# Sliding windows by DMA alone: 13 staged batches instead of 11, copies in 32 KB packets, and an exact last store

## The chip, the core and the metric

The kernel runs on one core of one Trainium2 chip. The metric is the device time of one execution in microseconds (us); lower is better. Three executions of the kernel before took 764.2, 765.02 and 766.24 us, so its median is 765.02 us. The profile comes from one further execution, which took 772.19 us.

## What is computed

Each of 32 batches of 4096 rows by 256 float32 values is cut into 127 windows of 64 rows, each window starting 32 rows behind the one before:

```python
batch, length, dim = (32, 4096, 256)
window_size, stride = 64, 32
n_windows = (length - window_size) // stride + 1      # 127
for i in range(n_windows):
    start = i * stride
    result[:, i] = x[:, start:start + window_size].copy()
```

No arithmetic is done. A batch is 128 blocks of 32 rows (one block is 32 KB). Window i is block i followed by block i+1, 64 KB in all. So every block but the first and the last of a batch is written twice: once as the second half of a window, once as the first half of the next. The input has 128 MB, the output 254 MB.

## The kernel before

Everything is done by DMAs on two rings: SP (SyncE) issues on one, which the profile calls q1, and ACT (ScalarE) on the other, q10. No compute engine touches the data. All DMAs go through `start` (L59), so line 60 stands for each of them; `parts=2` limits a packet to 32 KB, without it a packet may have 64 KB.

There are two ways for a batch to get from the input to the output.

- **Copied batches** (21 of 32, on q1, `copy`, L91): straight from device memory to device memory, as whole windows. Three DMAs per batch: windows 0 to 63 (`WHOLE`) in packets of 64 KB, windows 64 to 111 in packets of 32 KB, and the last 15 windows in packets of 32 KB.
- **Staged batches** (11 of 32, the odd ones from 1 to 21, on q10): one load of the 128 blocks into an on-chip tile, one block for each partition (`load`, L73), then two stores of that tile (`store`, L81), one that puts block j into the first half of window j, one that puts it into the second half of window j-1. There are five tiles (`BUFS`).

Both stores use all 128 blocks although a batch has 127 windows. So each staged batch also writes half a window too much on either side: its last block lands in the first half of the first window of the next batch, and its first block in the second half of the last window of the batch before. These neighbours have to be right in the end, in one of two ways:

- Tied batches (0, 2, ... 16): SP waits until both staged neighbours are stored (`after_store`, L71) and copies the batch only then.
- Early batches (18, 20, 22): they are copied first of all, and the halves that staged neighbours spoil are copied once more at the end ("mends", L151 to L155, five DMAs of 32 KB, each as 16 packets of 2 KB). Before the mends SP waits for the stores of staged batches 17, 19 and 21 (L147 to L149) and for the early copies (L150). ACT likewise waits for the early copies ahead of the first store that spoils one (L142).

The order of q1 is made by `_order` (L99): early batches, then the free ones (23 to 31) with the tied ones put in between. It gives 18, 20, 22, 23, 0, 24, 2, 25, 4, 26, 6, 27, 8, 28, 10, 29, 12, 30, 14, 31, 16. The order of q10 is load 0, then for each n: load n+1, wait for load n, store n. A load into a used tile waits for the store that read it. At the end SP waits for all stores and copies (L156 to L158) and clears the semaphores.

Of the kernel before, what the change touches and what calls it, by code (L numbers as in the profile page):

```python
# [1 line left out]

# [4 lines left out]


STAGED = tuple(range(1, 22, 2))
BUFS = 5  # L10

WHOLE = 64

EARLY = (18, 20, 22)


class _Geometry:


    def __init__(self, x, out, W, S):  # L20
        self.B, self.L, self.D = x.shape
        self.x, self.out = x, out
        self.n_win = (self.L - W) // S + 1
        self.n_blk = self.L // S
        self.blk = S * self.D
        self.win = W * self.D
        assert W == 2 * S and self.n_blk == self.n_win + 1 == 128

    def src(self, b, block, dims):

        at = (b * self.n_blk + block) * self.blk
        return bass.AP(self.x.tensor, self.x.offset + at, dims)

    def dst(self, b, half, dims):

        at = b * self.n_win * self.win + half * self.blk
        return bass.AP(self.out.tensor, self.out.offset + at, dims)

    def rows(self, b, w0, n):

        s, d = [[self.blk, n], [1, self.win]], [[self.win, n], [1, self.win]]
        return self.dst(b, 2 * w0, d), self.src(b, w0, s)

    def half(self, b, half, block):

        dims = [[self.blk // 16, 16], [1, self.blk // 16]]
        return self.dst(b, half, dims), self.src(b, block, dims)


class _Kernel:  # L50
    def __init__(self, nc, g, tiles):
        self.nc, self.g, self.tiles = nc, g, tiles
        self.loaded = [nc.alloc_semaphore(f"loaded{i}") for i in range(len(tiles))]
        self.stored = [nc.alloc_semaphore(f"stored{i}") for i in range(len(tiles))]
        self.copied = nc.alloc_semaphore("copied")
        self.early = nc.alloc_semaphore("early")
        self.count = {}

    def start(self, engine, out, in_, sem, parts=1):  # L59
        engine.dma_start(out=out, in_=in_, max_dma_last_dim=65536 // parts).then_inc(sem, 16)  # L60
        self.count[id(sem)] = self.count.get(id(sem), 0) + 16

    def all_of(self, engine, sem):
        engine.wait_ge(sem, self.count[id(sem)])

    def slot(self, n):
        return divmod(n, len(self.tiles))

    def after_store(self, engine, n):
        turn, i = self.slot(n)  # L70
        engine.wait_ge(self.stored[i], 32 * (turn + 1))  # L71

    def load(self, n):  # L73

        g, (_, i) = self.g, self.slot(n)
        if n >= len(self.tiles):
            self.after_store(self.nc.scalar, n - len(self.tiles))
        src = g.src(STAGED[n], 0, [[g.blk, g.n_blk], [1, g.blk]])
        self.start(self.nc.scalar, self.tiles[i][:, :], src, self.loaded[i])

    def store(self, n):  # L81

        g, (turn, i) = self.g, self.slot(n)
        self.nc.scalar.wait_ge(self.loaded[i], 16 * (turn + 1))
        for half in (0, -1):
            dst = g.dst(STAGED[n], half, [[g.win, g.n_blk], [1, g.blk]])
            self.start(self.nc.scalar, dst, self.tiles[i][:, :], self.stored[i])

    def copy(self, b, sem):  # L91

        n, nc = self.g.n_win, self.nc
        self.start(nc.sync, *self.g.rows(b, 0, WHOLE), sem)
        self.start(nc.sync, *self.g.rows(b, WHOLE, n // 16 * 16 - WHOLE), sem, 2)
        self.start(nc.sync, *self.g.rows(b, n // 16 * 16, n % 16), sem, 2)


def _order(B):  # L99


    near = {b for s in STAGED for b in (s - 1, s + 1)}
    order = list(EARLY) + [b for b in range(B) if b not in near and b not in STAGED]
    tied = sorted(near - set(EARLY))
    n = len(order) + len(tied)
    for b in tied:
        behind = max(STAGED.index(s) for s in (b - 1, b + 1) if s in STAGED)
        order.insert(-(-(behind + 2) * n // len(STAGED)), b)
    return order


@with_exitstack
def kernel(
    ctx: ExitStack,
    tc: tile.TileContext,
    x: bass.AP,
    window_size: bass.AP,
    stride: bass.AP,
    out: bass.AP,
):  # L120
    nc = tc.nc
    W, S = int(window_size), int(stride)
    g = _Geometry(x, out, W, S)
    assert 0 not in STAGED and g.B - 1 not in STAGED
    pool = ctx.enter_context(tc.tile_pool(name="blocks", bufs=1))
    tiles = [pool.tile([g.n_blk, g.blk], x.dtype, name=f"xb{i}") for i in range(BUFS)]

    with tc.tile_critical():
        k = _Kernel(nc, g, tiles)
        for b in _order(g.B):  # L130
            if b not in EARLY:
                for s in (b - 1, b + 1):
                    if s in STAGED:
                        k.after_store(nc.sync, STAGED.index(s))
            k.copy(b, k.early if b in EARLY else k.copied)
        k.load(0)
        waited = False
        for n, s in enumerate(STAGED):
            if n + 1 < len(STAGED):
                k.load(n + 1)  # L140
            if not waited and (s - 1 in EARLY or s + 1 in EARLY):
                k.all_of(nc.scalar, k.early)  # L142
                waited = True
            k.store(n)


        for n, s in enumerate(STAGED):  # L147
            if s - 1 in EARLY or s + 1 in EARLY:
                k.after_store(nc.sync, n)  # L149
        k.all_of(nc.sync, k.early)  # L150
        for b in EARLY:  # L151
            if b - 1 in STAGED:
                k.start(nc.sync, *g.half(b, 0, 0), k.copied)
            if b + 1 in STAGED:
                k.start(nc.sync, *g.half(b, 2 * g.n_win - 1, g.n_blk - 1), k.copied)  # L155
        for n in range(len(STAGED)):  # L156
            k.after_store(nc.sync, n)
        k.all_of(nc.sync, k.copied)  # L158
        for sem in [*k.loaded, *k.stored, k.copied, k.early]:
            nc.sync.sem_clear(sem)  # L160


# [1 line left out]
_INS = ['x', 'window_size', 'stride']  # L164
_OUTS = [((32, 127, 64, 256), 'float32')]

_NUMBERS = {'window_size': 64, 'stride': 32}


# [26 lines left out]
```

## Time and profile before

| what | value |
|---|---|
| median of three executions | 765.02 us |
| the profiled execution | 772.19 us |
| its span in the profile | 770.4 us |
| bytes moved by the 16 DMA engines | 313.37 MB, 407 GB/s over the span |
| device memory read and written | 221.09 MB and 267.22 MB |
| stretch 20 to 735 us | DMA engines busy 100%, 416 GB/s |
| stretch 735 to 762 us | DMA engines busy 88%, 313 GB/s |
| stretch 762 to 770.4 us | DMA engines busy 9%, 35 GB/s |

The only busy instructions of a compute engine are four memsets of 0.1 us each, so the profile's list of groups and its chain are empty in this kernel. What can be read are the DMA part of the page (share of the 16 engines' time for each queue, and what they move in 40 slices), the issues with their time to landing, the waits of SP, and the trace's record of each packet, with its queue, size, start and duration.

By these records, a 32 KB packet takes 1211 ns at least, and 1213 ns in the median, on either queue. All 32 KB packets of q1 take 1254.2 ns in the mean (2646 packets), those of q10 1259.6 ns (4224), and the 64 KB packets of q1 2583.8 ns (1344); the commonest fast duration of these is 2418 ns. Each DMA also leaves a record of 4 bytes on each engine that it uses, 9 ns long. In the mean 16.05 packets are on record at a time in the middle of the run, where there are 16 engines.

### The profile page before, as it was taken

How to read it: one execution, taken by the hardware profiler on the slowest of the kernel's cores; microseconds unless marked ns; L12 is line 12 of the kernel's file. 1: busy time of each engine (PE TensorE's matmuls, PEld its weight loads, DVE VectorE, ACT ScalarE, POOL GpSimd, SP SyncE). 2: the span in 40 equal slices, each digit the busy share in tenths (PEclk: the TensorE clock that was granted, in tenths of full speed). 3: DMA queues.
4: the chain of work that ended last, by engine and by line, in shares of the span. 5: the costliest groups of instructions: out<-in, count | busy, mean ns of one | idle time of the engine just before them, and what ended most of it. 6: DMA issues, size and time to landing. Idle time of an engine off the chain costs nothing. (4 is left out here: it accounts for less than half of the span.)

```text
span 770.4 us, 179 instructions
## 1 busy us (share of the span) xinstructions
POOL 0.2 (0%) x4
## 2 busy tenths in 40 slices
POOL 0000000000000000000000000000000000000000
DMA  9999999999999999999999999999999999999994
GB/s 381 396 412 436 393 413 419 447 371 434 400 424 395 441 403 424 403 444 386 430 420 422 405 419 419 403 412 419 417 415 427 417 415 412 444 415 432 391 338 178
DMA packets 9890, 313.37 MB, mean 407 GB/s; under 512 B 1595, under 2 KB 1595, under 8 KB 1675
## 3 DMA queue, kind: packets, MB, share of 16 engines
q1 hardware_dynamic: 5137, 174.95, 55.3%
q10 hardware_dynamic: 4752, 138.41, 43.2%
q14 instruction: 1, 0.01, 0.0%
HBM read 221.09 MB, written 267.22 MB: 634 GB/s over the span
## 5 line engine op out<-in xcount | busy, mean ns | idle before, releaser
L177 POOL MEMSET const-bfloat16-1.0<- 128x1 bf16 x1 | 0.1, 101 | 0.0
L177 POOL MEMSET const-uint8-127<- 128x1 uint8 x1 | 0.1, 101 | 0.0
L177 POOL MEMSET const-float32-0.0<- 128x1 f32 x1 | 0.1, 98 | 0.2 <-issue 0.2
L177 POOL MEMSET const-float32-1.0<- 128x1 f32 x1 | 0.1, 98 | 0.0
## 6 DMA issues: line engine op xcount, KB each, us to landing
out_dram<-xb ACTq DMA_DIRECT2D x22, 4096.0 KB, 94.1
out_dram<-in_x_dram SPq DMA_DIRECT2D x21, 3072.0 KB, 118.5
xb<-in_x_dram ACTq DMA_DIRECT2D x11, 4096.0 KB, 129.6
out_dram<-in_x_dram SPq DMA_DIRECT2D x21, 960.0 KB, 124.8
out_dram<-in_x_dram SPq DMA_DIRECT2D x21, 111.2
out_dram<-in_x_dram SPq DMA_DIRECT2D x5, 32.0 KB, 23.1
```

What stands on the lines that cost most here:

```text
L177: nc = _bacc.Bacc("TRN2", target_bir_lowering=False, num_devices=1)
```

## The change

- `STAGED` becomes 1, 3, ... 25: 13 staged batches and 19 copied ones.
- `copy` loses `WHOLE`: one DMA for windows 0 to 111 and one for the last 15, both in packets of 32 KB.
- The last staged batch (25) is stored by a new function, `store_exactly`. It leaves out the half windows that do not belong to the batch: each half is stored by one DMA of 112 rows and one of 15.
- `EARLY` becomes 20, 22, 24, 26. The mends are issued as soon as the stores of staged batches 19, 21 and 23 have landed, one staged batch after the other, and no longer behind the store of the last staged batch. Batch 26 needs no mend, since 25 writes nothing beyond its own windows.
- `_order` puts a tied batch half a place later. The order of q1 is now 20, 22, 24, 26, 0, 27, 2, 4, 28, 6, 8, 10, 29, 12, 14, 30, 16, 18, 31.

```diff
-STAGED = tuple(range(1, 22, 2))
+STAGED = tuple(range(1, 26, 2))
-WHOLE = 64
-EARLY = (18, 20, 22)
+EARLY = (20, 22, 24, 26)
...
+        self.exact = nc.alloc_semaphore("exact")
...
+    def store_exactly(self, n):
+        g, (turn, i) = self.g, self.slot(n)
+        self.nc.scalar.wait_ge(self.loaded[i], 16 * (turn + 1))
+        whole = g.n_win // 16 * 16
+        for half in (0, 1):
+            for w, rows in ((0, whole), (whole, g.n_win - whole)):
+                dst = g.dst(STAGED[n], 2 * w + half, [[g.win, rows], [1, g.blk]])
+                src = self.tiles[i][w + half : w + half + rows, :]
+                self.start(self.nc.scalar, dst, src, self.exact)
+
     def copy(self, b, sem):
-        n, nc = self.g.n_win, self.nc
-        self.start(nc.sync, *self.g.rows(b, 0, WHOLE), sem)
-        self.start(nc.sync, *self.g.rows(b, WHOLE, n // 16 * 16 - WHOLE), sem, 2)
-        self.start(nc.sync, *self.g.rows(b, n // 16 * 16, n % 16), sem, 2)
+        whole = self.g.n_win // 16 * 16
+        self.start(self.nc.sync, *self.g.rows(b, 0, whole), sem, 2)
+        self.start(self.nc.sync, *self.g.rows(b, whole, self.g.n_win - whole), sem, 2)
...
-        order.insert(-(-(behind + 2) * n // len(STAGED)), b)
+        order.insert(-(-(2 * behind + 5) * n // (2 * len(STAGED))), b)
...
-            k.store(n)
-        for n, s in enumerate(STAGED):
+            (k.store if n < last else k.store_exactly)(n)
+        k.all_of(nc.sync, k.early)
+        for n, s in enumerate(STAGED[:last]):
             if s - 1 in EARLY or s + 1 in EARLY:
                 k.after_store(nc.sync, n)
-        k.all_of(nc.sync, k.early)
-        for b in EARLY:
-            if b - 1 in STAGED:
-                k.start(nc.sync, *g.half(b, 0, 0), k.copied)
-            if b + 1 in STAGED:
-                k.start(nc.sync, *g.half(b, 2 * g.n_win - 1, g.n_blk - 1), k.copied)
-        for n in range(len(STAGED)):
+            if s - 1 in EARLY:
+                k.start(nc.sync, *g.half(s - 1, 2 * g.n_win - 1, g.n_blk - 1), k.copied)
+            if s + 1 in EARLY:
+                k.start(nc.sync, *g.half(s + 1, 0, 0), k.copied)
+        for n in range(last):
             k.after_store(nc.sync, n)
+        k.all_of(nc.sync, k.exact)
         k.all_of(nc.sync, k.copied)
```

## The prediction

> **What bounds the kernel now.** I read first the page's DMA slices and its queues, since no compute engine works.
>
> ```profile
> DMA  9999999999999999999999999999999999999994
> GB/s 381 396 412 436 393 413 419 447 371 434 400 424 395 441 403 424 403 444 386 430 420 422 405 419 419 403 412 419 417 415 427 417 415 412 444 415 432 391 338 178
> ...
> q1 hardware_dynamic: 5137, 174.95, 55.3%
> q10 hardware_dynamic: 4752, 138.41, 43.2%
> ```
>
> All 16 DMA engines are busy to the end, and the queues hold 55.3 + 43.2 = 98.5% of their time. So time is bytes per engine times time per byte, and no wait counts unless it empties a ring. The slices swing between 371 and 447 GB/s: the time per byte is not constant. Next the waits of SP's queue:
>
> ```profile
> SPq L71 <- DMA out_dram<-xb: 601.5, 9, 97.0
> SPq L60 <- DMA out_dram<-xb: 85.8, 1, 85.8
> SPq L64 <- DMA out_dram<-in_x_dram: 26.3, 1, 26.3
> ```
>
> SP waits for stores nearly all the time, yet the engines never pause before 735 us: copies issued earlier cover these waits. Only the last 26.3 us (L64, all copies landed) is bare. The windows show the end:
>
> ```profile
> 20.00:735.00 715.00, 0.00 (x0) 1.00 1.00 416
> 735.00:762.00 27.00, 0.00 (x0) 1.00 0.88 313
> 762.00:770.40 8.40, 0.00 (x0) 1.00 0.09 35
> ```
>
> (columns: window, length, POOL, clock, DMA share, GB/s.) By the packet records q10's data ends at 736 us, q1's at 767.9; the engines end one by one, most between 758 and 764. One engine falls out at 710 already: it has no share in the DMAs of 15 windows.
>
> **The work of one engine**, before, for the 15 engines that set the end. A copied batch is 4 packets of 64 KB (64 windows / 16), 6 of 32 KB (48 x 2 / 16) and 2 (the last 15 windows): 512 KB. A staged batch is 8 + 8 + 8 packets of 32 KB: 768 KB. In all 21 x 512 + 11 x 768 = 19,200 KB, as 84 packets of 64 KB, 168 copied and 264 staged of 32 KB. At the mean durations: 84 x 2583.8 = 217.0, 168 x 1254.2 = 210.7, 264 x 1259.6 = 332.5, sum 760.3 us. The records overlap a little (16.05 at a time on 16 engines), so the true work is 760.3 / 1.003 = 758.1. The span closes: 2.2 until the first packet, 758.1, 7.6 from the mean engine to the last one with the small records, 2.5 from the last packet to the end: 770.4.
>
> At the fast durations the same packets would take 84 x 2.418 + 432 x 1.213 = 727.1 us. So 31 us are slowing, and the change is a trade of more bytes against less slowing.
>
> **Part 1, two batches from copied to staged.** 19 x 512 + 13 x 768 = 19,712 KB: one engine gets 512 KB more, all in 32 KB packets, 19 x 16 = 304 copied and 13 x 24 = 312 staged (the exact store has 14 + 2, as many as a plain one). Fast: 616 x 1.213 = 747.2 us, that is **+20.1 us**. Of these 0.7 us are the split of 84 large packets (2 x 1213 - 2418 = 8 ns each).
>
> **Part 2, the time of a packet.** From 25 to 735 us I cut the packet records into slices of 5 us. Where 64 KB packets are under 2% of the bytes (28 slices) the engines move 425.5 GB/s, where they are over 60% (35 slices) 400.7, all together 415.8. Staged bytes are 51% of the first kind and 32% of the second, so size and share of copies can't be told apart, but the change alters both towards the first kind: its staged share is 312/616 = 51%. 425.5 / 16 = 26.6 GB/s, or 1232 ns for 32 KB. A second reading: 32 KB packets that overlap no 64 KB packet take 1234.8 ns (copies) and 1246.3 (staged), mean 1240.6, over 1.003 1237. The lower end is the fast packet, 1213, which some stretches hold; the upper end is today's mean of all 32 KB packets, (304 x 1254.2 + 312 x 1259.6) / 616 / 1.003 = 1253. I take 1228, a little under both readings, because the copy's DMA of 64 windows, whose engines stand 4 windows apart, goes, and the engines of the new one stand 7 apart. 616 x 1.228 = 756.4: against the 758.1 of now **-1.7 us** for parts 1 and 2 together. Ends: 747.2 (-10.9) and 771.8 (+13.7).
>
> The row for that choice is 400.7 against 425.5 GB/s in the two kinds of slices. [...]
>
> **Part 3, the balance of the rings.** Each engine seems to take a packet of either ring in turn, the 4-byte record of each DMA too. Before, q1 has 21 x (12 + 3) = 315 turns, q10 11 x (24 + 3) = 297. So q10 should end with 18 turns of q1 left, some 14 data packets of 42.7 KB in the mean, 14 x 1.7 = 24 us; q1 ended 32 us behind q10, and q10 began 4.4 us ahead. The rule holds about. After: q1 19 x (16 + 2) + 5 mends x 2 = 352, q10 12 x 27 + 9 + 20 = 353. Both end together, with some 4 packets left for q10's early start. What the lone ring costs now: 32 KB packets behind 741 us take 1402 ns, 64 KB ones 3085. That is inside the means above, so nothing more is booked; the 7.6 us to the last engine I keep, with bounds of -4 and +4.
>
> **Part 4, waits.** q1 must never run dry while SP waits for a store. Store n ends at turn 27n + 36 of q10; when SP waits for it, 18 turns for each copy issued stand in q1. Batch 0 waits for store 0 with 72 turns issued against 36 run; the closest are batches 10, 14 and 18: 198 against 171, 252 against 225, 306 against 279. 27 turns are 24 packets, with as many of q10 between them: 48 x 1.23 = 59 us of cover. Without it, each microsecond of lateness leaves SP's ring empty and the staged ring alone. ACT's order is unchanged: while it waits for load n, store n-1 and load n+1 stand in the ring. Its wait for the early copies (four now, landing near turn 72, about 160 us) moves to n = 9, past 500 us, at nothing. Five buffers stay. SP issues 43 DMAs instead of 68 at about 0.6 us each, 15 us less on a queue that waits 600: nothing.
>
> **Part 5, mends and the last store.** Before, the five mends land 23.1 us after their issue, because q1's last copies stand ahead of them:
>
> ```profile
> out_dram<-in_x_dram SPq DMA_DIRECT2D x5, 32.0 KB, 23.1
> ```
>
> So their lateness costs nothing now. After, the last two are issued when store 11 lands, 20 turns before q10's end, about 16 x 2 x 1.23 = 39 us, behind some 15 turns of q1: they land ahead of the end. Were they still behind the last store, a bare landing of a few us would stand there. The exact store of 112 partitions is a form that the trace does not show. Its 16 packets per engine cost 1213 ns at least; the slowest stretch of 20 us has staged packets of 1356 ns: 16 x 0.128 = +2.0. I take +0.5, near a plain store. Small records: 101 an engine before, 84 after, at 9 ns: -0.2. [...]
>
> **Sum.** -1.7 + 0.5 - 0.2 = -1.4 us on the span: 769.0. The profiled execution took 772.19, 7.2 more than the median; I take the difference, not the level: 765.0 - 1.4 = **763.6 us**.
>
> **Rivals.**
> 1. *More bytes at the old pace* (slower). The slowing is of the memory, whatever the packet's size and ring, and 32 KB packets keep 1253 ns: 765.0 + 13.7 = 779 us. It decides from a mean of 1234 ns on (616 x 1.234 = 760.2, +2.1). For it: staged packets between none and eight 64 KB packets show 1246, 1240 and 1235 ns, no rise. Against it: 1272 ns with nine or more, and the 28 slices.
> 2. *Slowing nearly gone*: most packets at 1213: 765.0 - 10.9 = 754 us. For it: three quarters of the 32 KB packets are at this floor today, and the GB/s slices reach 447. Against it: the pure slices still average 425.5, not 432.
> 3. *The rings are not level* (slower): a ring runs out early because turns do not count as I think. If the 4-byte records took no turn, 304 stand against 312, 8 packets alone. If SP falls behind its 59 us, the hole is whole: 10 us would make 775. Against it: the 24 us worked out against 32 seen.
>
> **How the numbers follow.** A measurement of this kernel tells about 0.3% (2.3 us) from no change, so same is 762.7 to 767.3. My forecast has 0.55, split 0.25 faster, 0.165 same, 0.135 slower, since 1225 or 1236 ns would both fit it (762 to 769 us). Rival 1 0.20, slower; rival 2 0.18, faster; rival 3 0.07, of it 0.05 slower. Faster 0.25 + 0.18 = 0.43, same 0.165 + 0.02 = 0.19 (rounded up), slower 0.38. The range reaches close to rival 2's end and two thirds of the way to rival 1's: 753 to 775; the forecast's own is 757 to 769.
>
> **What would show it.** The page should have about 321.9 MB (19 x 8.32 + 13 x 12.58 + 0.2, less 0.1), 418 to 421 GB/s over the span, q1 and q10 near 49 and 50% of the engines, even slices without the swing of now, and both queues' data ending within 10 us of each other; the last bare wait of SP should be for the exact store or the copies, a few us. A 32 KB mean over 1240 ns shows rival 1, one at 1215 rival 2. Dips of the DMA share before 740 us would show rival 3. The prediction is wrong if the mean is near 1228 ns and the span still is not near 769: then the ends or a dry ring took the difference.

## The result, and the profile after

The changed kernel took 773.38 us (median of four executions, 772.0 to 774.32) beside 765.63 us of the kernel before (four executions, 764.2 to 766.87): a ratio of 1.010 with a 95% interval of 1.0073 to 1.0128. It is slower by 1%, clear of the interval. The forecast was 763.6 us and slightly faster; the measured time lies in its range of 753 to 775, on the other side of no change.

The DMA part of the page of the changed kernel, with its 40 slices, its queues (packets, MB, share of the 16 engines' time) and the traffic of device memory:

```profile
DMA  9999999999999999999999999999999999999994
GB/s 380 431 407 434 433 417 433 419 422 434 426 422 434 421 417 434 426 422 431 419 429 429 431 417 433 424 419 433 431 419 431 431 424 433 424 426 416 414 381 154
...
q10 hardware_dynamic: 5644, 163.51, 50.1%
q1 hardware_dynamic: 5575, 158.30, 48.4%
HBM read 212.83 MB, written 267.29 MB: 621 GB/s over the span
```

The swing of the slices is gone (407 to 434 in the middle, 371 to 447 before), and the rings share the engines evenly. In stretches of time:

```profile
20.00:735.00 715.00, 0.00 (x0) 1.00 1.00 425
735.00:753.00 18.00, 0.00 (x0) 1.00 0.95 383
753.00:762.00 9.00, 0.00 (x0) 1.00 0.87 288
762.00:772.50 10.50, 0.00 (x0) 1.00 0.12 42
```

(columns as in the prediction: window, length, POOL, clock, DMA share, GB/s.) The long stretch moves 425 GB/s where it moved 416, a gain of 2.2%, but 321.83 MB are to be moved instead of 313.37, 2.7% more. The end is still 30 us of falling rate. The waits of SP:

```profile
SPq L70 <- DMA out_dram<-xb: 506.9, 9, 59.8
SPq L59 <- DMA out_dram<-xb: 186.4, 3, 74.5
SPq L63 <- DMA out_dram<-xb: 35.9, 1, 35.9
...
SPq L63 <- DMA out_dram<-in_x_dram: 0.2, 1, 0.2
```

Before, the last bare wait was for the copies (26.3 us). Now it is for the exact store (35.9 us, where the prediction had a few us), and q1 is down 0.2 us later: counted in turns, the two rings end together, as foretold. Counted in data they do not. By the packet records the last 32 KB packet of a copy ends at 754.5 us and the last of the staged ring at 769.4; between them q1 has only its mends, 2 KB at a turn. The prediction had the two queues' data within 10 us of each other. By the same records the copies' 32 KB packets take 1238.1 ns in the mean, the staged ones 1240.9; those of the exact store alone 1416, the other staged ones 1231.5.

### The profile page after: what moved, and what is told of

It is laid out like the page before. It is cut to its first block, busy times and chain, and to the rows that moved or that the text cites. A ratio compares the mean times of both kernels' runs of the same rounds, so it can differ in the third digit from the quotient of the medians.

```text
span 772.5 us, 164 instructions
## 1 busy us (share of the span) xinstructions
POOL 0.2 (0%) x4
## 2 busy tenths in 40 slices
DMA packets 11220, 321.83 MB, mean 417 GB/s; under 512 B 1323, under 2 KB 1323, under 8 KB 1403
## 3 DMA queue, kind: packets, MB, share of 16 engines
q10 hardware_dynamic: 5644, 163.51, 50.1%
```

## The experiments

Theory A stood at first: the 512 KB more for each engine cost 20 us, and the slowing that the change removes is worth less than that. Theory A also took the profiled execution of the kernel before for a slow one. Its rivals: a profile adds 7 us to it (B), the 32 KB packets are the harm (C), the exact store is the harm (D). Ratios are to the kernel before on the same chip. The runs went to four chips, and on all of them the kernel before took 769.6 to 774.4 us.

### The kernel before once more (ctl_before)

No edit.

> The kernel before, unchanged, profiled once more. Theory A (the level of the one profiled execution was high: 31 us of slowing against some 24 in an ordinary one): the new profile has a span near 764 us, 32 KB packets of 1240 to 1250 ns and 64 KB packets of 2520 to 2560 instead of 1254, 1260 and 2584. Rival B (a profile adds 7 us to this kernel): span near 770 and the same packet means again. The timed ratio is 1.00 under both.

771.49 us, ratio 1.0005 (0.9992 to 1.0019). The new profile has a span of 770.2 us, and its packets take 1256.4, 1260.3 and 2586.4 ns: those of the first profile again. Timed executions without a profile are no faster (20 executions, 769.71 to 774.4). So A's number fails, and B's as well: it is neither a high profile nor the profiling. On these four chips some 771 to 772 us is this kernel's ordinary time, and the four executions at 764 to 767 us are the exception.

### The changed kernel once more (after_again)

No edit; run later, when theory A had become A' (below).

> The changed kernel unchanged, timed beside the kernel before on the same chip. Theory A' (two ceilings: the kernel before sits at the rate of device memory, about 645 GB/s read and written, the changed one at the rate of the DMA engines, 27 GB/s each; the engines' rate is fixed, the memory's differs between placements, so before moves between 765 and 772 us and the changed kernel does not): before 770 to 772, changed 772 to 775, ratio 1.001 to 1.005. Rival (a fixed cost of 1%): 778 us, ratio 1.010.

774.65 us (twelve executions) against 771.43: ratio 1.0047 (1.0031 to 1.0063). So the change costs about 0.5% on this chip, and the first comparison's 1.0% has another 0.5% in it that lies in the time of the kernel before, since the changed kernel moved by only 1.3 us. Why those four executions were faster was not found; no run reproduced them. The reason that theory A' gives in its expectation, a rate of device memory that differs from place to place, is a guess that no run here tests.

### Packet size alone, both ways (b_copies32, a_copies64)

11 staged batches with the new copy; 13 with the old one.

```diff
 # b_copies32: the kernel before
-        self.start(nc.sync, *self.g.rows(b, 0, WHOLE), sem)
-        self.start(nc.sync, *self.g.rows(b, WHOLE, n // 16 * 16 - WHOLE), sem, 2)
-        self.start(nc.sync, *self.g.rows(b, n // 16 * 16, n % 16), sem, 2)
+        whole = self.g.n_win // 16 * 16
+        self.start(self.nc.sync, *self.g.rows(b, 0, whole), sem, 2)
+        self.start(self.nc.sync, *self.g.rows(b, whole, self.g.n_win - whole), sem, 2)
 # a_copies64: the changed kernel, with the opposite edit
```

> 11 staged batches as before, but all copies in 32 KB packets. Bytes per engine stay at 19,200 KB. Theory A (only bytes and the overall mix of copies set the time, packet size does not): the two rings run level at about 1235 ns a packet until q10 ends some 80 packets ahead of q1, then copies alone at about 1400: 520 x 1.235 + 80 x 1.40 = 754 us of work, 762 to 768 us timed, ratio 0.995 to 1.003. Rival C (32 KB packets are what makes the changed kernel slow): 772 or more, ratio 1.008 or more. The other way, if 64 KB packets were the harm before: 750 to 757, ratio under 0.99.

> The changed kernel with the copies of before (64 windows in 64 KB packets). Theory A (the 512 KB more per engine are the cost): 772 to 778 us, ratio 1.009 to 1.017, with a tail of q10 alone. Rival C (packet size): 764 to 768, ratio about 1.00.

b_copies32: 775.07 us, ratio 1.005 (1.0036 to 1.0064), between A's range (up to 1.003) and C's (from 1.008). a_copies64: 793.47 us, ratio 1.0279 (1.0257 to 1.0301), where A had 1.009 to 1.017 and C about 1.00. Neither had the cause. The windows of both, b_copies32 first:

```profile
20.00:669.00 649.00, 0.00 (x0) 1.00 1.00 423
669.00:762.00 93.00, 0.00 (x0) 1.00 0.94 324
762.00:773.20 11.20, 0.00 (x0) 1.00 0.24 100
```

```profile
20.00:650.00 630.00, 0.00 (x0) 1.00 1.00 417
650.00:737.00 87.00, 0.00 (x0) 1.00 0.99 415
737.00:792.10 55.10, 0.00 (x0) 1.00 0.80 278
```

In b_copies32 the staged data ends at 669.6 us and copies run alone for 100 us at 324 GB/s. In a_copies64 the copies end at 735.6 us and the staged ring runs alone for 54, at 278 GB/s; before that, q1 was empty three times for 7 to 10 us (from 414, 533 and 654 us on): SP was waiting for a store and issued the next copies only at 419, 539 and 659. In the changed kernel neither ring has a gap over 1.4 us between 25 and 735 us.

So the packet size acts through the rings. If each engine takes a packet or a 4-byte record of either ring in turn, as the prediction's part 3 supposes, a staged batch brings 768 KB in 27 turns and a copied one 512 KB in 18 with 32 KB packets, in 15 with the old copy. The staged share of the bytes is then 0.500 or 0.455. From 20 to 650 us it is 0.500 in b_copies32 and 0.501 in the changed kernel, 0.454 in the kernel before; only a_copies64, with its empty q1, is off, at 0.48. The size that fits 11 staged batches does not fit 13: with 13, the 32 KB packets are worth 793.5 - 774.7 = 19 us (two chips; 18 by the ratios), with 11 they cost 4. No harm of the size itself is seen: over that stretch b_copies32 and a_copies64 read and write 638 and 635 GB/s of device memory. Rival C falls.

### The last store (a_plain_last, only_staged, only_staged_plain)

The changed kernel with `k.store(n)` for the last batch too, whose two neighbours are then mended behind it:

```diff
-            (k.store if n < last else k.store_exactly)(n)
+            k.store(n)
...
-        for n, s in enumerate(STAGED[:last]):
+        for n, s in enumerate(STAGED):
...
```

> The changed kernel with a plain last store: batch 25 spoils a half window of 24 and 26, which are mended behind it. Theory A (bytes): the exact store's packets of 1416 ns fall to some 1240, 16 x 0.17 = 2.8 us less, and a bare landing of the two last mends comes back, 2 to 3 us: 771 to 774 us, ratio 1.007 to 1.011. Rival D (the exact store is what makes the change slow): 765 to 768, ratio 1.00 to 1.003.

773.64 us, ratio 1.0028 (1.0015 to 1.0041), 1.0 us under after_again, with intervals that overlap; A had a ratio of 1.007 to 1.011, D one up to 1.003. It meets D's only because the changed kernel itself is at 1.0047 here and not at 1.010. The packets of its last store take 1213 ns in the mean. What that saves is paid again at the end: the last store lands at 766.65 us, and SP issues two mends behind it and waits for them:

```profile
734.79 33.03 SPq L59 DMA_DIRECT2D out_dram<-in_x_dram  x4
SPq L63 <- DMA out_dram<-in_x_dram: 1.1, 1, 1.1
```

(the first line, of the timeline: four mends, two issued from 734.8 us on and two up to 767.8; the second, of the waits, starts only behind them.) They land at 769.31, 2.7 us behind the store. The store's own cost was also taken by itself, with only the staged batches (copies and mends are left out), with the exact and with the plain last store:

> The copies and the mends are left out: only the 13 staged batches of the changed kernel, q10 alone, 312 packets per engine. [...] If staged transfers slow each other: 1235 ns or more outside the exact store, 396 us.

> As only_staged (copies and mends left out), and with the plain last store. If the exact form alone slows its packets: the last store's packets fall from 1646 ns to about 1215, the span from 395.7 us by 16 x 0.43 = 7 us to 387 to 390. If the end of a lone ring is slow whatever the form: no change.

The spans are 395.7 and 388.3 us, of one execution each. The windows of only_staged, then of only_staged_plain:

```profile
20.00:340.00 320.00, 0.00 (x0) 1.00 1.00 430
340.00:395.70 55.70, 0.00 (x0) 1.00 0.88 327
```

```profile
20.00:340.00 320.00, 0.00 (x0) 1.00 1.00 430
340.00:388.20 48.20, 0.00 (x0) 1.00 0.88 378
```

The loads and the other stores take 1224 ns in both; the last store's packets 1646 ns exact and 1213 plain. So the form costs 16 x 0.43 = 7 us an engine by itself and 16 x 0.18 = 2.9 us beside copies. In a_plain_last the 2.7 us of the late mends take its place, so 1 us or less shows in the whole time. Rival D's cost is real. It does not explain the first 1.0%, but it is nearly the 3.2 us by which the changed kernel is slower in after_again; that a last store without either cost would make the two kernels equal (774.7 - 2.9 = 771.8 us) is an estimate, and no run has such a store. Why a store from 112 and 15 partitions takes longer than one from 128, no run here shows.

### Copies alone, and where they lie (all_copied32, all_inter32)

No batch is staged; then the same with neighbouring windows on neighbouring engines (shortened: in the kernels this is a helper, `spread`):

```diff
-        self.start(self.nc.sync, *self.g.rows(b, 0, whole), sem, 2)
+        for p in (0, 1):
+            d = [[g.win, 16], [16 * g.win, whole // 16], [1, g.blk]]
+            s = [[g.blk, 16], [16 * g.blk, whole // 16], [1, g.blk]]
+            self.start(self.nc.sync, g.dst(b, p, d), g.src(b, p, s), sem, 2)
```

> No batch is staged: 32 copies, q1 alone, 266.3 MB, 16,384 KB per engine or 512 packets of 32 KB. By the lone tail of before (32 KB packets 1402 ns): 512 x 1.40 = 718 us of work, 727 us timed, ratio 0.95; if with all engines in step copies run at 350 GB/s: 761 us plus 10, ratio 1.00. Theory A says that staging saves slowing and costs bytes, so the result lies between 720 and 775 us. Rival E (device memory traffic alone sets the time, 634 GB/s as before): 532 MB / 634 = 839 us, ratio 1.09.

> All 32 batches copied, none staged, with neighbouring windows on neighbouring engines. Memory alone binds here (326 GB/s in all_copied32, 818.6 us). If the pattern matters it shows here most: 790 us or less, or 850 or more; if not, 815 to 822.

818.64 us (ratio 1.0604, 1.0578 to 1.063) and 818.43 us (1.0607, 1.0583 to 1.0631). The page of all_copied32:

```profile
GB/s 303 332 318 331 331 331 331 326 329 321 329 321 334 329 332 328 328 336 328 331 329 331 328 331 324 332 326 324 326 331 334 331 321 332 328 324 329 326 331 265
...
q1 hardware_dynamic: 9120, 266.34, 98.2%
HBM read 266.34 MB, written 266.34 MB: 652 GB/s over the span
```

Theory A, which had 720 to 775 us, falls here. Rival E, with device memory alone, had 839, from the 634 GB/s of the kernel before. The engines are busy (DMA share 0.99 from 20 to 780 us) and the rate is flat at 329 GB/s, with 1577 ns for a 32 KB packet where the staged ones of only_staged have 1224. A copy's byte is read from and written to device memory, a staged byte touches it once (on the pages, 266.34 MB read and 266.34 written here, 54.53 and 108.99 for the 163.51 MB of only_staged). So 329 GB/s of copies are 657 GB/s of device memory. The engines themselves do not need longer for a copy: beside staged transfers, in the changed kernel, the same packets of copies take 1238 ns. So what binds is shared by the 16 engines, and the traffic of device memory fits it; reads and writes, or the number of copies at a time, were not varied apart.

Standing 1 window apart instead of 7, the engines have 1576 ns against 1577. That speaks against the reason given in the prediction for taking 1228 ns, though 4 windows apart, as in the kernel before, were not run against 7 by themselves.

### The same spreading in both kernels (a_inter, b_inter)

> The changed kernel, but in the copy's 112 windows neighbouring windows go to neighbouring engines, so that the 16 engines read and write 16 windows that lie side by side, where before they stood 7 apart; each half window is a DMA of its own. Theory A' (engine rate binds): no more than the 11 us of slowing can go, 764 to 775 us. If the memory's ceiling depends on the pattern and the pattern is worse: over 780.

> The kernel before with the same spreading of the copies' windows over the engines (64 windows in 64 KB packets, 48 in 32 KB by halves). Theory A' (memory's rate binds before): if side by side helps the memory, 745 to 760 us, ratio 0.97 to 0.985; if it does not, 769 to 776; if worse, over 780, a larger change than in the changed kernel.

777.64 us (1.0074, 1.0056 to 1.0092) and 776.54 us (1.0063, 1.0047 to 1.0079). Both are a little slower than their originals, and both lie just over what A' had for a spreading without effect (775 and 776): spreading helps neither. In both, the extra DMA of each copy gives q1 one turn more per batch, and the staged ring ends earlier (761.5 us against 768.0 in after_again, 711.1 against 735.3 in ctl_before), so they compare the pattern and the balance together.

### Fewer and twelve staged batches (staged9_64, staged12_level)

```diff
 # staged9_64: the kernel before
-STAGED = tuple(range(1, 22, 2))
+STAGED = tuple(range(1, 18, 2))
-WHOLE = 64
+WHOLE = 112
-EARLY = (18, 20, 22)
+EARLY = (14, 16, 18)
...
-        self.start(nc.sync, *self.g.rows(b, WHOLE, n // 16 * 16 - WHOLE), sem, 2)
 # staged12_level: the changed kernel with the old copy
-STAGED = tuple(range(1, 26, 2))
+STAGED = tuple(range(1, 24, 2))
+WHOLE = 48
-EARLY = (20, 22, 24, 26)
+EARLY = (18, 20, 22, 24)
```

> Nine staged batches (1 to 17), the copies' 112 windows in 64 KB packets: the other way from the change. Bytes per engine 23 x 512 + 9 x 768 = 18,688 KB, 512 KB less than before; turns 23 x 11 + 10 = 263 against 243, so the rings are nearly level. Theory A: 20 us less at the fast pace, and a staged share of 37% instead of 44% brings slowing back, 404 GB/s by the slices of before: 304.6 MB / 404 = 754 plus 10, 760 to 768 us, ratio 0.993 to 1.003. If slowing grew as the bytes fall or faster, 768 to 780.

> The changed kernel with 12 staged batches (1 to 23), early batches 18, 20, 22, 24, and 48 windows of each copy in 64 KB packets, so that the rings stay level: 20 x 16 + 10 = 330 turns against 11 x 27 + 29 = 326. Theory A' (two ceilings): 317.6 MB, staged share 0.475, memory at 640 GB/s gives 640 / 1.525 = 420 GB/s, 756 us of transfer as in both kernels, 770 to 774 us timed, ratio 0.998 to 1.004: the optimum is flat. Rival F (level rings were missing before and two more staged batches are the cost): 762 to 767, ratio under 0.995.

staged9_64: 777.1 us, ratio 1.006 (1.0038 to 1.0082). Theory A had 760 to 768 us and misses again; the time lies in the other case of the expectation, slowing that grows as the bytes fall. staged12_level: 772.93 us, ratio 1.0013 (0.9999 to 1.0026): as A' had it, and rival F falls. Between 9 and 13 staged batches with the rings about level, all times lie within 0.8% of the kernel before.

By the packet records of the long middle (20 to 650 us; copies alone to 780, staged alone to 340), with the staged share f of the bytes, and device memory as rate x (2 - f):

| kernel | GB/s by the engines | f | GB/s of device memory |
|---|---|---|---|
| all_copied32 | 328.6 | 0 | 657 |
| staged9_64 | 400.4 | 0.380 | 649 |
| before (first profile) | 415.1 | 0.454 | 642 |
| after_again | 424.5 | 0.501 | 636 |
| only_staged | 430.1 | 1 | 430 |

From top to bottom the rate of device memory falls from 657 to 430 GB/s, while the engines go from 76% of their fastest rate (16 x 32,768 B / 1213 ns = 432 GB/s) to 99.5%. This is theory A': two ceilings, 657 GB/s of device memory, as copies alone have it, and 432 GB/s of the engines. They cross near f = 0.5, where 432 x 1.5 = 648. It is a rough picture: taking the lower of the two, staged9_64 should have 406 GB/s, the kernel before 425 and after_again 432, and they have 1 to 2% less. But it is nearer than the plain rival that each kind of packet takes its own time wherever it runs: that would give 361, 368 and 373.

## Why the prediction was wrong

The forecast of 763.6 us was 9.8 too low: 3.5 us in the span (769.0 foretold, 772.5 in the profile) and 6.3 in the level, the step from the profiled execution to the others. The mechanism of the sum held; two of its terms, the packet's time and the exact store, were mis-sized, and the step of the level failed.

- **Part 1, the bytes**: right. 616 packets an engine, 321.83 MB on the page (321.9 foretold).
- **Part 2, the time of a packet**: the mechanism was right and the size was off by 3 ns. Without the exact store, packets take 1234.8 ns in the profile of the changed kernel ((296 x 1231.5 + 304 x 1238.1) / 600), over 1.003 1231, where 1228 was taken and the slices had said 1232: 600 x 3 ns = +1.9 us. The reason for going below the slices, that the engines now stand 7 windows apart, was a guess, and no run shows the 1228; all_inter32 shows no effect for 1 window against 7 (1576 ns and 1577). The slices were no finer than that either: with each packet shared out over the slices that it covers, those almost free of 64 KB packets have 424.6 GB/s, 1235 ns.
- **Part 5, the exact store**: mis-sized. +0.5 was booked, and 16 x (1416 - 1232) = +2.9 us measured in the first profile. The row it was set beside, staged packets of plain stores at 1356 ns, has nothing of this form's cost, and no run shows the +0.5.
- **The ends**: 7.6 us were kept from the mean engine to the last. In the changed kernel 772.5 - 1.9 - 761.3 - 3.0 leaves 6.3 (761.3 is 304 x 1238.1 + 312 x 1240.9 over 1.003), so -1.3.
- Together the span should have been 769.0 and was 772.5: +1.9 + 2.4 - 1.3, and 0.5 more from the end of the program. That turns the -1.4 of the forecast into +2.1 us, and with it the sign. This step of the prediction failed: a sum of -1.4 between terms of 20 was worked out with two guesses of its own size, both taken on the favourable side. In the profile of after_again (span 770.9) the same terms read +4.3 (packets of 1238.9 ns, over 1.003 1235), +2.0 (exact store 1393) and -4.8 (ends): the signs hold and the span is again longer than before (770.4), not shorter, but single terms differ by up to 3.5 us between two profiles of one kernel.
- **The level**: this is the largest miss. The difference of 7.2 us between the profiled execution and the median was carried over to the changed kernel. The repeats show that the profiled execution was the ordinary one. The changed kernel's profiled execution is 0.9 us above its median, 6.3 less than booked. A prediction of the changed kernel's own level, 769.0 + 1.8 outside the span = 770.8, would have been 2.6 us off instead of 9.8.
- **Part 3, the balance**: right in its rule and its end (rings down 0.2 us apart by SP's waits). The turns give the staged share of the bytes in the long middle within 0.002 in the kernel before (0.455, measured 0.454), staged9_64 (0.379, 0.380), staged12_level (0.471, 0.472), a_inter (0.514, 0.513) and b_inter (0.471, 0.472). Without a turn for the 4-byte records the kernel before would have 0.429. What is left over at the end comes out only roughly: for b_copies32 some 80 lone packets, and 100 us at the 1529 ns that its lone copies take are 65. Not foreseen was that the mends fill q1's last turns with little data, so that the exact store ran all but alone for 15 us.
- **Part 4, no dry ring**: right; neither ring has a gap over 1.4 us between 25 and 735 us. The DMA share of 1.00 alone would not show it: a_copies64 has that share over the time in which its q1 was empty. **Mends**: right; the last one is down 0.2 us behind the exact store. In a_plain_last, where two come behind the last store, they land 2.7 us after it, the few us foretold.
- **Rival 1**, the slower case, had the right side for a wrong reason: 32 KB packets did not stay at 1253 ns. Their mean is 1236 with the exact store, past the 1234 from which this rival was to decide, and 1231 without it. It is not the slowing that stayed; the 16 packets more cost as much as its going saved (616 x 1.231 = 758.3 us, 758.1 before). **Rival 2** fell, 1231 ns is far from 1213. **Rival 3** did not occur in the changed kernel; a_copies64 shows what it costs: 54 us of a lone ring and 19 us of time.

What is shown: the change raises the middle rate about as much as it adds bytes, so both kernels need about as long there (313.4 MB / 415 GB/s = 755 us; 321.8 MB at the 426 and 424.5 GB/s of the two profiles of the changed kernel = 755 and 758), and its exact store costs 2.9 us on top of a plain one. What is argued from the table: before, the kernel lies near the memory's ceiling; changed, it lies near where the two meet. Open: what let the kernel before run in 764 to 767 us in its first four executions, and so about half of the first comparison's 1.0%.

## What to carry to other kernels

When one kind of transfer is bound by device memory and another by the DMA engines, rate both against both ceilings (here 329 GB/s of copies alone, 430 of staged alone) and look where the mix meets them. Near that crossing the optimum was flat here: from 9 to 13 staged batches, moving work from one kind to the other bought nothing (with the rings about level, all times lie within 0.8%). The two rings shared the engines packet by packet, so packet size set their shares (with 11 staged batches, 0.454 of the bytes were staged beside the old copy and 0.500 beside copies in 32 KB packets); change it together with the work in each ring, or one will run on alone. Before a sum of one or two us is trusted, repeat the baseline: its level here moved by 6 us.

## What was not expected of the hardware

- The exact store, from 112 and 15 partitions, took 1646 ns in the mean for a 32 KB packet by itself, the store from 128 took 1213.
- A DMA's 4-byte record, 9 ns long, took a whole turn of its ring: with it the staged share of the kernel before comes out as 0.455 (0.454 measured), without it as 0.429.
- Copies alone, with all 16 engines busy, took 1577 ns a packet, 12% more than the 1402 seen in the lone tail of the kernel before, and the one other spacing of the windows that was run did not change it (1576).
